# Hybrid GLA / sliding-window layer on one core: second FF product in groups of eight, decayed keys made earlier, and a new order at two Strassen seams

## The chip, the core and the metric

The kernel runs on one core of a Trainium2 chip. TensorE (PE) multiplies, VectorE (DVE), ScalarE (ACT) and GpSimd (POOL) do the elementwise work, SyncE (SP) issues every DMA. The metric is the time of one execution in microseconds of device time; the figure for a kernel is the median of its runs.

## What is computed

One decoder layer over 2048 tokens of width 1024, in float32, with 16 learned meta tokens ahead of them:

```python
u = rmsnorm(h, norm_mix_w); proj = u @ w_in
o_gla = gla_mixer(gq, gk, gv, gr, glr, ...)   # 4 heads, gated linear attention in chunks
o_swa = swa_mixer(sq, sk, sv, sinks, pos)     # 8 heads, window 128, 16 meta keys, a sink
h = h + concat([o_gla, o_swa]) @ w_out
f = rmsnorm(h, norm_ff_w)
h = h + square(relu(f @ w_ff1)) @ w_ff2       # 1024 -> 4096 -> 1024
return rmsnorm(h, final_norm_w)
```

Within a chunk of GLA the state is S = exp(b_last) S + sum over j of (k_j exp(b_last - b_j)) v_j. The factor k_j exp(b_last - b_j) is what the kernel calls the decayed keys.

## The kernel before

**Layout.** Activations lie transposed, 128 features on the partitions and 512 tokens (a block, `NB`) along the free axis; four blocks make up the 2048 tokens. Every dense product is done in split precision: an operand x is kept as a rounded part h and a rest l = x - h, and `mm3` issues three matmuls (wh·ah, wl·ah, wh·al; lines 160, 161, 162) where one would do. Weights arrive as 128x1024 tiles (`raw`, 512 KB); ACT makes `wh`, DVE `wl` (`split_w`, lines 125 and 126). A product of K row tiles is 3K matmuls of 512 columns into one PSUM bank (`psd`, three banks in rotation).

**Stages in order.** (1) `in_proj`, blocks 0 and 1, then 2 and 3. (2) `trunk(0)` and `trunk(1)`: output projection, first FF product (`up`, 32 FF tiles), second FF product (`down`). (3) `tail_pair`, blocks 2 and 3 together: the output projections, then in `tail_ordered` a cover of dense work and the first FF product by a Strassen scheme of seven products per 2x2 of tiles (operands `ops[1..7]`), 16 rounds j of seven slots, 12 matmuls a slot. (4) the class `Second`: the second FF product by the same scheme, 49 steps of 24 matmuls. (5) `last_down`, a plain remainder, and the final norm.

**What runs beside the dense work.** From stage 1 into stage 2 two generators are advanced once per `yield` of the dense code: `gla` (chunks of 128 tokens) and `swa`. Their matmuls stand among the dense ones on PE; a scheduler that plans ahead of time decides the order on each engine up to the end of the output projections of stage 3. Each engine runs its list in order, so a PE instruction that waits holds all that stand behind it. A GLA chunk makes seven levels (`gla_level`, `gla_level_mm`; `kl`, `ql`, `lv`), whose key tiles alternate between two buffers `kl[0]` and `kl[1]`; the decayed keys are put into `kl[1]` too, after the last level.

**The FF pair.** `up(ff)` writes one hidden tile pair; `down(g)` multiplies a group of four of them for all eight output tiles m and adds each product to the residual `hs[m]` on DVE (line 863). The pairs live in a pool `hb` of five units. In the last group of block 0 and the sixth of block 1 the inputs of the next output projection are loaded and split as well (`ahead`, `load_mix`).

**The cover and the first Strassen rounds.** The last eight FF tiles of block 1 (`hid6`, `hid7`) are not used in `trunk(1)`. `tail_ordered` multiplies them in 16 products of 12 matmuls, and under this cover DVE and ACT build the first Strassen operands from a list `chain`, in pieces that `work(us)` hands out by nominal DVE costs (1.23 us for a 128x1024 subtraction). From here to the end the order on every engine is the order of the code (`manual_schedule`). The products of a round go to four banks b0 to b3. Line 1264 forms c11 = s + b2; slot 6 of the round accumulates into b2 again, so its first matmul waits for that read.

**The second product.** `Second` has a table of jobs by step (`job(at, ...)`). `prepare(s)` makes `wh` and `bh` on ACT, `wl` and `bl` on DVE; it runs two steps ahead, for steps 0 and 1 inside the last Strassen round (`before(slot)`). A step works on four PSUM banks, one after another, `psw`: three of the pool that also holds b0 and b2 (`pd`), one of `px`. `close_0` (line 1195) is the last read of the last round's b2. `load_acc` loads the residual sums `c21`, `e`, `f`, `c11`; `sum_acc` forms f = e - f and e = e - c21.

Of the kernel before, what the change touches and what calls it, by code (L numbers as in the profile page):

```python
# [35 lines left out]
class Layer:  # L36
# [546 lines left out]
    def decayed_keys(self, gp, B, k, n):  # L583

        nc = self.nc
        kt = self.kl[1][:, :, :n]
# [100 lines left out]
    def gla_chunk(self, b, gp, qk, v):  # L687
# [30 lines left out]
        kt = self.decayed_keys(gp, B, k, P)  # L718
        yield
        kT = self.transpose_keys(gp, kt, P)  # L720
# [96 lines left out]
    def trunk(self, blk, ahead_of, hid_pair, last):  # L817
# [14 lines left out]
        hid = [[None] * 4 for _ in range(8)]  # L832

        def up(ff):
# [10 lines left out]
            hid[ff // 4][ff % 4] = (h, l)  # L845
# [9 lines left out]
        def down(g):  # L855
            if g == 7:
                accs[0] = self.acc_tile()
            for mp in range(4):
                w = self.split_w(a["w2"][g, mp].rearrange("p m k c -> p (m k c)"))
                for mi in range(2):  # L860
                    m = 2 * mp + mi
                    ps = yield from self.product(w, lambda k: hid[g][k], 4, 4 * mi)
                    nc.vector.tensor_tensor(hs[m], hs[m], ps, ALU.add)  # L863
                    if g == 7:
                        self.sumsq_add(hs[m], accs[0], m, fast=True)
                    if g == (5 if last else 7) and m >= 4:
                        self.ahead = self.ahead or ahead_of()
                        for _ in range(3):
                            next(self.ahead[0], None)
                    yield  # L870

        yield from up(0)
        for g in range(8):
            for t in range(1, 4):
                yield from up(4 * g + t)
            if g < 7:
                yield from up(4 * g + 4)
            if last and g >= 6:
                continue
            self.half_way = last and g >= 5  # L880
# [5 lines left out]
        if last:  # L886
            self.left = hs, units, hid[6], hid[7]
# [4 lines left out]
    def tail_pair(self, blks, ax, hb, pq):  # L892
# [3 lines left out]
        hs1, units1, hid6, hid7 = self.left  # L896
# [58 lines left out]
        def cov_load(t):  # L955
            cov_raw[t] = self.wp.tile([P, 1024], F32, name="raw", tag="raw")
            nc.sync.dma_start(out=cov_raw[t], in_=a["w2"][6 + t // 4, t % 4].rearrange("p m k c -> p (m k c)"))
# [19 lines left out]
    def tail_ordered(  # L977
# [3 lines left out]
        hs1, units1, hid6, hid7 = self.left  # L981
# [130 lines left out]
        def cov_add(m, last, ps):  # L1112
            TT(hs1[m], hs1[m], ps, ALU.add)
            if last and m % 2:
# [565 lines left out]
```

## Time and profile before

| | |
|---|---|
| median of 3 runs | 2188.69 us (2186.64 to 2188.81) |
| the profiled execution, its own time | 2190.38 us |
| span of that execution, first to last instruction | 2188.7 us |
| mean granted TensorE clock | 0.994 of full speed |
| PE busy | 2149.2 us, 98% of the span |
| DVE busy | 1575.0 us, 72% |
| ACT busy | 1047.6 us, 48% |

Matmuls overlap: a 512-column matmul is shown as 0.39 us long, and the next one starts 0.227 us after it. So where PE runs without a gap its time is the number of matmuls, and the questions are where it stands idle and where the next start comes later than 0.227 us.

### The profile page before, as it was taken

Reading aid. Unit: us, or ns where it says so; the run is one execution under the profiler, and the core shown is the slowest. Engines: PE = TensorE matmul, PEld = TensorE weight load, DVE = VectorE, ACT = ScalarE, POOL = GpSimd, SP = SyncE. Lnnn points to the kernel's source line nnn. Section 1 sums busy time; section 2 is a strip of 40 time slices with the busy share of each in tenths; the row PEclk is TensorE's granted clock in tenths of the full one; section 3 lists DMA queues with packets and bytes.
Section 4 is the critical chain, followed back from the end, with each engine's and each line's share of the span. In section 5 each row is a group of like instructions: output and inputs, shape, how many; then the busy total and the mean of one; then the engine's idle time right before and its main releaser. Section 6 shows DMA issues by size and latency. Waiting matters only on the chain.

```text
span 2188.7 us, 29186 instructions
## 1 busy us (share of the span) xinstructions
PE 2149.2 (98%) x10423; PEld 1804.3 (82%) x10423; DVE 1575.0 (72%) x2927; ACT 1047.6 (48%) x2156; POOL 193.7 (9%) x311
## 2 busy tenths in 40 slices
PE   8999999999999999999999999999999999999997
PEld 6998789788888888887888888888788887888886
DVE  6167774988988888889974445566867775775866
ACT  5132754456665556667553323453544444333434
POOL 2000110121221111221110000000000000000001
PEclk9999999999999999999999999999999999999999
DMA  6234533335333333334333334553355557654412
GB/s 205 96 98 133 152 112 110 100 114 171 109 104 99 103 110 109 106 102 146 126 100 98 96 97 146 176 166 129 119 162 176 169 197 251 254 173 144 154 39 77
DMA packets 146801, 291.47 MB, mean 133 GB/s; under 512 B 12256, under 2 KB 63968, under 8 KB 146656
## 3 DMA queue, kind: packets, MB, share of 16 engines
q1 hardware_dynamic: 146656, 289.61, 41.4%
q8 instruction: 82, 1.34, 0.3%
q14 instruction: 63, 0.52, 0.1%
HBM read 219.63 MB, written 69.86 MB: 132 GB/s over the span
## 4 chain that ended last, share of the span: by engine, by line
PE 84%; DVE 8%; ACT 4%; DMA 2%; issue 1%; POOL 0%; DVEq 0%; SPq 0%; ACTq 0%; POOLq 0%
PE psd L161 15%; PE psd L160 15%; PE psd L162 15%; PE psq L160 4%; PE psq L161 4%; PE psq L162 4%; PE psw L160 4%; PE psw L162 4%; PE psw L161 4%; PE lv L677 2%; PE psd L295 2%; PE psd L296 2%; PE psd L297 2%; PE pv L530 1%; ACT p L479 1%
## 5 line engine op out<-in xcount | busy, mean ns | idle before, releaser
L125 ACT ACTIVATE wh<-raw 128x1024 fp32r<-128x1024 f32 (+2 forms) x190 | 199.2, 1048 | 322.6 <-PE psd L162 279.6
L126 DVE TENSOR_TENSOR wl<-raw,wh 128x1024 fp32r<-128x1024 f32 (+2 forms) x190 | 233.9, 1231 | 75.3 <-ACT wh L125 74.4
L160 PE MATMUL psd<-hid,wh 128*128 128x512 f32 x512 | 203.7, 398 | 0.2 <-ACT hid L843 0.2
L160 PE MATMUL psd<-f,wh 128*128 128x512 f32 x512 | 202.7, 396 | 0.0
L162 PE MATMUL psd<-f,wh 128*128 128x512 f32 x512 | 200.2, 391 | 0.0
L161 PE MATMUL psd<-f,wl 128*128 128x512 f32 x512 | 199.9, 390 | 0.0
L161 PE MATMUL psd<-hid,wl 128*128 128x512 f32 x512 | 199.8, 390 | 0.0
L162 PE MATMUL psd<-hid,wh 128*128 128x512 f32 x512 | 199.6, 390 | 0.0
L160 PE MATMUL psd<-u,wh 128*128 128x512 f32 x416 | 169.2, 407 | 4.9 <-DVE st L241 3.2
L161 PE MATMUL psd<-u,wl 128*128 128x512 f32 x416 | 164.7, 396 | 1.0 <-DVE wl L126 1.0
L162 PE MATMUL psd<-u,wh 128*128 128x512 f32 x416 | 165.0, 397 | 0.3 <-DVE u L156 0.2
L160 PE MATMUL psw<-bh,wh 128*128 128x512 f32 x392 | 153.2, 391 | 2.1 <-DVE su L1195 2.1
L161 PE MATMUL psw<-bh,wl 128*128 128x512 f32 x392 | 153.2, 391 | 0.0
L162 PE MATMUL psw<-bl,wh 128*128 128x512 f32 x392 | 153.1, 391 | 0.0
L161 PE MATMUL psq<-oh,wl 128*128 128x512 f32 x384 | 149.5, 389 | 0.8 <-DVE wl L963 0.8
L162 PE MATMUL psq<-ol,wh 128*128 128x512 f32 x384 | 149.6, 390 | 0.6 <-DVE ol L913 0.6
L160 PE MATMUL psq<-oh,wh 128*128 128x512 f32 x384 | 149.8, 390 | 0.0
L962 ACT ACTIVATE wh<-rw 128x1024 fp32r<-128x1024 f32 x49 | 52.0, 1061 | 150.5 <-PE psw L162 134.3
L863 DVE TENSOR_TENSOR h<-h,psd 128x512 f32<-128x512 f32 x112 | 76.6, 684 | 61.4 <-PE psd L162 61.1
L162 PEld LDWEIGHTS psd<-f,wh 128*128 128x128 f32 x512 | 96.1, 188 | 21.1 <-DVE f L156 0.4
L162 PEld LDWEIGHTS psd<-hid,wh 128*128 128x128 f32 x512 | 96.1, 188 | 20.6
L160 PEld LDWEIGHTS psd<-hid,wh 128*128 128x128 f32 x512 | 96.2, 188 | 19.7 <-ACT hid L843 0.4
(315 smaller groups left out, 5229.4 us busy)
## 6 DMA issues: line engine op xcount, KB each, us to landing
raw<-w SPq DMA_DIRECT2D x132, 512.0 KB, 3.6
b<-hops SPq DMA_DIRECT2D x49, 512.0 KB, 3.5
raw<-wo SPq DMA_DIRECT2D x32, 512.0 KB, 4.0
r<-w SPq DMA_DIRECT2D x32, 512.0 KB, 4.0
rw<-w2q SPq DMA_DIRECT2D x28, 512.0 KB, 5.5
raw<-wf SPq DMA_DIRECT2D x26, 512.0 KB, 3.7
feat<-st SPq DMA_DIRECT2D x52, 256.0 KB, 2.2
hops<-t SPq DMA_DIRECT2D x42, 256.0 KB, 5.0
```

The source lines that it names most:

```text
L125: nc.scalar.activation(wh, raw, AF.Copy)
L126: nc.vector.tensor_tensor(wl, raw, wh.bitcast(F32), ALU.subtract)
L160: nc.tensor.matmul(ps, lhsT=wh, rhs=ah, start=first, stop=False, skip_group_check=skip)
L161: nc.tensor.matmul(ps, lhsT=wl, rhs=ah, start=False, stop=False, skip_group_check=skip)
L162: nc.tensor.matmul(ps, lhsT=wh, rhs=al, start=False, stop=last, skip_group_check=skip)
L295: nc.tensor.matmul(ps, lhsT=ah, rhs=wh, start=kt == 0, stop=False)
L296: nc.tensor.matmul(ps, lhsT=ah, rhs=wl, start=False, stop=False)
L297: nc.tensor.matmul(ps, lhsT=al, rhs=wh, start=False, stop=kt == KT - 1)
L479: nc.scalar.activation(p[:, g, win], p[:, g, win], AF.Exp, bias=nm[:, g : g + 1], accum_out=sm[:, g : g + 1])
L677: nc.tensor.matmul(ps[:, hp * P : (hp + 1) * P], lhsT=kl[:, hp, :], rhs=ql[:, :, hp, :], start=True, stop=True)
L863: nc.vector.tensor_tensor(hs[m], hs[m], ps, ALU.add)
L962: nc.scalar.activation(wh, src, AF.Copy)
```

## The change

Four edits, of which the first alters the weights' layout, too:

1. `down` works on groups of eight FF tiles (24 matmuls into one bank, one addition to `hs[m]`) instead of four; the cover does the same with `hid3`, the last eight tiles, one output tile at a time. Nine hidden pairs live at once: five in `hb`, four in the pool of the activations (`ap_`).
2. The decayed keys get a tile of their own and are made at level 3 and transposed at level 5, no longer behind level 6.
3. In the cover, `work` hands out 0.80 and 2.72 us in turn where it handed out 0.80 and 2.03.
4. In the second product, `prepare` is cut into a high and a low half. In the last Strassen round the low half of step 0 comes after the reads of slot 5, that of step 1 after `close_0`. The four banks of a set are taken in the order pd, pd, px, pd (before: pd, pd, pd, px). The loads of `e`, `f` move from step 0 to steps 5 and 7, `c11` from 5 to 4; a copy `x` of the original `c21` is loaded at step 6 into `hb`, and `sum_acc` moves from steps 2 and 3 to 12 and 13.

```diff
     def decayed_keys(self, gp, B, k, n):
-        kt = self.kl[1][:, :, :n]
+        kt = gp.tile([P, 2, P], F32, name="kt", tag="g", bufs=1)[:, :, :n]
...
             yield
+            if li == 3:
+                kt = self.decayed_keys(gp, B, k, P)
+            elif li == 5:
+                kT = self.transpose_keys(gp, kt, P)
             self.gla_level_mm(li, AT, *lv[li])
...
-        kt = self.decayed_keys(gp, B, k, P)
         yield
-        kT = self.transpose_keys(gp, kt, P)
         yield
...
         def down(g):
...
-            for mp in range(4):
-                w = self.split_w(a["w2"][g, mp].rearrange("p m k c -> p (m k c)"))
-                for mi in range(2):
-                    m = 2 * mp + mi
-                    ps = yield from self.product(w, lambda k: hid[g][k], 4, 4 * mi)
-                    nc.vector.tensor_tensor(hs[m], hs[m], ps, ALU.add)
...
+            for m in range(KT):
+                w = self.split_w(a["w2"][g, m].rearrange("p k c -> p (k c)"))
+                ps = yield from self.product(w, lambda k: hid[g][k])
+                nc.vector.tensor_tensor(hs[m], hs[m], ps, ALU.add)
+                if g == 3:
+                    self.sumsq_add(hs[m], accs[0], m, fast=True)
+                if g == (2 if last else 3) and m >= 4:
...
         for i in range(16):
-            g, m = i // 8, i % 8
+            m, half = i // 2, i % 2
...
-            for k, (h, l) in enumerate((hid6, hid7)[g]):
...
+            for k in range(4 * half, 4 * half + 4):
+                c = slice(k * P, (k + 1) * P)
+                self.mm3(ps, wh[:, c], wl[:, c], *hid3[k], k == 0, k == 7)
...
-                work(2.72 - 0.69 - (1.23 if i % 2 == 0 else 0))
+                work(2.72 - (1.92 if half == 0 else 0))
...
         close_0(old)
+        W2.prepare_lo(1)
...
-                    lambda ff: self.pair("hid", F32R, self.ap_ if ff >= 29 else hb),
+                    lambda ff: self.pair("hid", F32R, hb if ff % 9 < 5 else self.ap_),
...
         self.job(-4, self.load_acc, "c21", 0, 1)
-        self.job(0, self.load_acc, "e", 1, 1)
-        self.job(0, self.load_acc, "f", 1, 0)
+        self.job(5, self.load_acc, "e", 1, 1)
+        self.job(6, self.load_acc, "x", 0, 1, hb)
+        self.job(7, self.load_acc, "f", 1, 0)
+        self.job(4, self.load_acc, "c11", 0, 0)
+        for s in range(2, len(self.steps)):
+            self.job(s - self.AHEAD, self.prepare, s)
...
-            self.job(2, self.sum_acc, "f", "e", "f", u)
-            self.job(3, self.sum_acc, "e", "e", "c21", u)
...
+            self.job(12, self.sum_acc, "f", "e", "f", u)
+            self.job(13, self.sum_acc, "e", "e", "x", u)
...
+        if slot == -4:
+            self.prepare_hi(0)
+        elif slot == -2:
+            self.prepare_lo(0)
+            self.prepare_hi(1)
...
-                banks[i].append(lay.px.tile([P, NB], F32, name="psw", tag="sx"))
+                banks[i].insert(2, lay.px.tile([P, NB], F32, name="psw", tag="sx"))
...
-    A["w2"] = f["w_ff2"][0].reshape(8, 4, P, 4, 2, P).transpose(0, 3, 2, 4, 1, 5)
+    A["w2"] = f["w_ff2"][0].reshape(4, 8, P, KT, P).transpose(0, 3, 2, 1, 4)
```

In the program that results, the list of PE holds the same number of each kind of matmul; DVE's holds 64 fewer additions of 128x512 (96 instead of 160 of the form h<-h,psd), SP's two more loads.

**Place 1: the transposes of the decayed keys (`kT`) in the fifth of 17 calls, during the in-projection of blocks 2 and 3.** On DVE, before:

```order
L682 COPY_PREDICATED AT<-lmask,lv 128x256
L717 TENSOR_TENSOR qB<-qk,eB 128x256
L587 TENSOR_TENSOR kl_123<-B 128x256
L126 TENSOR_TENSOR wl<-raw,wh 128x1024
L589 TENSOR_TENSOR kl_123<-kl_123,qk 128x256
```

and with the change, where the level of size 4 stands around it:

```order
L587 TENSOR_TENSOR kt<-B 128x256
L659 TENSOR_TENSOR E<-B 128x256
L663 TENSOR_TENSOR kl_122<-qk,E 128x32x4
L667 TENSOR_TENSOR ql<-qpad,E 128x256
L589 TENSOR_TENSOR kt<-kt,qk 128x256
L243 TENSOR_TENSOR st<-psd,rb 128x512
```

On PE `kT` stood between two matmuls of the sliding window, 15 matmuls behind the last level's `lv`; now it stands ahead of the level of size 2, at least 12 dense matmuls behind the `lv` that reads the `ql` above:

```order
L160 MATMUL psd<-u,wh 128x512
L161 MATMUL psd<-u,wl 128x512
L162 MATMUL psd<-u,wh 128x512
L596 MATMUL kT<-tabs,kt 128x128 x2
L677 MATMUL lv<-ql,kl_123 128x128 x2
```

**Place 2: DVE from the end of the cover into the first Strassen round.** L1113 is the cover's addition, L913 makes the low part `ol` of an operand, L1046 and L1049 are sums of operands, L963 is a `wl`. Before, from the last addition to the read of b2 (L1264):

```order
L1113 TENSOR_TENSOR h<-h,psd 128x512
L1046 TENSOR_TENSOR h<-h 128x1024
L963 TENSOR_TENSOR wl<-x,wh 128x1024
L913 TENSOR_TENSOR ol<-t_14343,oh 128x1024
L1046 TENSOR_TENSOR h<-h 128x1024
L913 TENSOR_TENSOR ol<-t_14384,oh 128x1024
L963 TENSOR_TENSOR wl<-r,wh 128x1024
...
```

With the change the same pieces begin ahead of the last addition (the second L1113 here):

```order
L1046 TENSOR_TENSOR h<-h 128x1024
L1113 TENSOR_TENSOR h<-h,psd 128x512
L963 TENSOR_TENSOR wl<-x,wh 128x1024
L913 TENSOR_TENSOR ol<-t_14221,oh 128x1024
L1046 TENSOR_TENSOR h<-h 128x1024
L1113 TENSOR_TENSOR h<-h,psd 128x512
L913 TENSOR_TENSOR ol<-t_14260,oh 128x1024
L963 TENSOR_TENSOR wl<-r,wh 128x1024
...
```

Behind these, on either side, follow two L1049, L1026, L1255 (now L1256), one L963 and several L913 (before five, now six: one has moved up from behind the pair), and then the pair L1263, L1264 (now L1264, L1265).

**Place 3: DVE at the seam of the two Strassen products.** L1263 and L1264 (now L1264, L1265) read the banks of slots 4 and 5, L1195 (now L1196) the last bank b2; L963 and L1562 (now L1567) are the low halves of `prepare`. Before:

```order
L963 TENSOR_TENSOR wl<-rw,wh 128x1024
L1562 TENSOR_TENSOR bl<-b,bh 128x1024
L1263 TENSOR_TENSOR su<-su,psq 128x512
L1264 TENSOR_TENSOR cc<-su,psq 128x512
L963 TENSOR_TENSOR wl<-rw,wh 128x1024
L1562 TENSOR_TENSOR bl<-b,bh 128x1024
L1266 TENSOR_TENSOR su<-su,psq 128x512
L1161 SCALAR_TENSOR_TENSOR h_16621<-h_16621,vecs,rb 128x512
L1195 TENSOR_TENSOR su<-su,psq 128x512
```

Now:

```order
L1264 TENSOR_TENSOR su<-su,psq 128x512
L1265 TENSOR_TENSOR cc<-su,psq 128x512
L963 TENSOR_TENSOR wl<-rw,wh 128x1024
L1567 TENSOR_TENSOR bl<-b,bh 128x1024
L1267 TENSOR_TENSOR su<-su,psq 128x512
L1162 SCALAR_TENSOR_TENSOR h_16510<-h_16510,vecs,rb 128x512
L1196 TENSOR_TENSOR su<-su,psq 128x512
L963 TENSOR_TENSOR wl<-rw,wh 128x1024
L1567 TENSOR_TENSOR bl<-b,bh 128x1024
```

The reads of the two banks moved ahead of all low halves, and the low half of step 1 behind the read of b2.

## Rows read from the trace of the kernel before

**Rows 1.** Page, part 1: busy us (share of the span) and instructions of each engine

```profile
PE 2149.2 (98%) x10423; PEld 1804.3 (82%) x10423; DVE 1575.0 (72%) x2927; ACT 1047.6 (48%) x2156; POOL 193.7 (9%) x311
```

**Rows 2.** Waits of PE, whole span: line, releaser, us in total, times, longest

```profile
PE kT L596 <- DVE kl L589: 4.8, 3, 3.0
...
PE psq L160 <- DVE cc L1264: 2.7, 2, 1.3
PE psw L160 <- DVE su L1195: 2.1, 1, 2.1
...
PE psq L161 <- DVE wl L963: 0.8, 1, 0.8
PE psq L162 <- DVE ol L913: 0.6, 1, 0.6
```

**Rows 3.** Windows: stretch, length, busy us of PE, PEld, DVE, ACT, POOL, clock, DMA

```profile
380.00:440.00 60.00, 56.20 (x287) 46.62 (x287) 56.92 (x139) 26.65 (x81) 10.75 (x18) 1.00 0.34 106
...
1000.00:1050.00 50.00, 46.86 (x232) 37.54 (x231) 47.91 (x104) 33.66 (x86) 8.52 (x16) 1.00 0.54 181
...
1545.00:1565.00 20.00, 18.04 (x71) 13.70 (x70) 19.90 (x22) 12.49 (x16) 0.00 (x0) 0.91 0.18 53
...
1845.00:1865.00 20.00, 16.50 (x65) 12.84 (x64) 10.22 (x11) 9.56 (x12) 0.00 (x0) 0.91 0.85 301
1865.00:2145.00 280.00, 280.00 (x1237) 231.91 (x1236) 201.38 (x205) 105.53 (x110) 0.00 (x0) 1.00 0.42 145
```

**Rows 4.** Timeline around the longest kT wait: start us, us, engine, line, operation, idle before

```profile
424.80 0.41 DVE L589 TENSOR_TENSOR kl<-kl,qk 128x256 f32<-128x256 f32 x1
...
425.36 0.41 PE L596 MATMUL kT<-tabs,kl 128*128 128x128 f32 x2 [2.99 <-DVE kl L589]
```

**Rows 5.** Groups by line, DVE: operation, shapes, count, busy us, mean ns, idle before

```profile
L863 DVE TENSOR_TENSOR h<-h,psd 128x512 f32<-128x512 f32 x112 | 76.6, 684 | 61.4 <-PE psd L162 61.1
```

**Rows 6.** Waits of PE, 60 to 1100 us (columns as in rows 2)

```profile
PE pv L530 <- POOL ph L523: 1.0, 1, 1.0
PE oT L766 <- DVE o L739: 0.9, 1, 0.9
```

**Rows 7.** Timeline of the first Strassen round, PE and DVE (columns as in rows 4)

```profile
1544.16 1.22 DVE L913 TENSOR_TENSOR ol<-t,oh 128x1024 fp32r<-128x1024 f32 x1
...
1556.71 2.36 DVE L913 TENSOR_TENSOR ol<-h,oh 128x1024 fp32r<-128x1024 f32 x2
1558.98 0.69 DVE L1263 TENSOR_TENSOR su<-su,psq 128x512 f32<-128x512 f32 x1
1559.70 0.69 DVE L1264 TENSOR_TENSOR cc<-su,psq 128x512 f32<-128x512 f32 x1
...
1560.54 0.57 PE L160 MATMUL psq<-oh,s 128*128 128x512 f32 x1 [1.35 <-DVE cc L1264]
1560.90 0.63 PE L161 MATMUL psq<-oh,s 128*128 128x512 f32 x1
...
1563.46 0.63 PE L161 MATMUL psq<-oh,s 128*128 128x512 f32 x1
```

**Rows 8.** Timeline at the seam of the two Strassen products (columns as in rows 4)

```profile
1847.63 1.23 DVE L1562 TENSOR_TENSOR bl<-b,bh 128x1024 fp32r<-128x1024 f32 x1 [3.25 <-PE psq L162]
...
1850.23 0.50 PE L160 MATMUL psq<-oh,s 128*128 128x512 f32 x1 [1.35 <-DVE cc L1264]
...
1856.02 0.68 DVE L1195 TENSOR_TENSOR su<-su,psq 128x512 f32<-128x512 f32 x1
...
1856.76 0.50 PE L160 MATMUL psw<-bh,wh 128*128 128x512 f32 x1 [2.15 <-DVE su L1195]
...
1857.84 0.63 PE L161 MATMUL psw<-bh,wl 128*128 128x512 f32 x1
...
1860.39 0.63 PE L161 MATMUL psw<-bh,wl 128*128 128x512 f32 x1
```

**Rows 9.** Page, part 6, a DMA of 2 KB runs: count, KB each, median us to landing

```profile
rw<-w2q SPq DMA_DIRECT2D x28, 512.0 KB, 5.5
```

More of the change, by code (lines that the diff above doesn't have):

```diff
@@ L831, in trunk @@
         rb = []
-        hid = [[None] * 4 for _ in range(8)]
+        hid = [[None] * 8 for _ in range(4)]
         def up(ff):
@@ L855, in down @@
         def down(g):
-            if g == 7:
+            if g == 3:
                 accs[0] = self.acc_tile()
-            for mp in range(4):
-                w = self.split_w(a["w2"][g, mp].rearrange("p m k c -> p (m k c)"))
-                for mi in range(2):
-                    m = 2 * mp + mi
-                    ps = yield from self.product(w, lambda k: hid[g][k], 4, 4 * mi)
-                    nc.vector.tensor_tensor(hs[m], hs[m], ps, ALU.add)
[L864 to L870, printed above, removed]
-        yield from up(0)
[L873 to L878, printed above, removed]
+            for m in range(KT):
+                w = self.split_w(a["w2"][g, m].rearrange("p k c -> p (k c)"))
+                ps = yield from self.product(w, lambda k: hid[g][k])
+                nc.vector.tensor_tensor(hs[m], hs[m], ps, ALU.add)
+                if g == 3:
+                    self.sumsq_add(hs[m], accs[0], m, fast=True)
+                if g == (2 if last else 3) and m >= 4:
+                    self.ahead = self.ahead or ahead_of()
+                    for _ in range(3):
+                        next(self.ahead[0], None)
+                yield
+        yield from up(0)
+        for g in range(4):
+            for t in range(1, 8):
+                yield from up(8 * g + t)
+            if g < 3:
+                yield from up(8 * g + 8)
+            if last and g == 3:
                 continue
-            self.half_way = last and g >= 5
+            self.half_way = last and g == 2
             yield from down(g)
@@ L886, in trunk @@
         if last:
-            self.left = hs, units, hid[6], hid[7]
+            self.left = hs, units, hid[3]
         else:
@@ L1134, in tail_ordered @@
                 cov_add(*adds)
-            adds = (m, g, ps)
+            adds = (m, ps) if half else None
             if i % 2 == 0 and i // 2 + 1 < 8:
@@ L1475, in __init__ @@
         self.job(-4, self.load_acc, "c21", 0, 1)
-        self.job(0, self.load_acc, "e", 1, 1)
-        self.job(0, self.load_acc, "f", 1, 0)
-        for u in range(2):
-            self.job(2, self.sum_acc, "f", "e", "f", u)
-            self.job(3, self.sum_acc, "e", "e", "c21", u)
-        self.job(5, self.load_acc, "c11", 0, 0)
-        for s in range(len(self.steps)):
-            self.job(s - self.AHEAD, self.prepare, s)
+        self.job(5, self.load_acc, "e", 1, 1)
[4 more added lines that the diff above has]
+            self.job(s - self.AHEAD, self.prepare, s)
+        for u in range(2):
+            self.job(12, self.sum_acc, "f", "e", "f", u)
+            self.job(13, self.sum_acc, "e", "e", "x", u)
         self.hid, self.ws, self.raw = [None] * 4, [None] * 8, {}
```

43 lines of the change are left out of this document (23 added, 20 removed).

## The prediction, made before the changed kernel ran

> **What bounds the kernel now.** I read the table of engines first. PE is busy 98% of the span [rows 1], so only idle time of PE or slow matmuls can be won back; the change leaves PE's matmul counts alone. In a stretch without a gap, 1237 matmuls take 280 us [rows 3], 0.227 us from start to start; a slot of 12 is then 2.72 us, a product of 24 is 5.45.
>
> Then the waits of PE. The three groups that stand behind the edited code are the transposes of the decayed keys, 4.8 us in three waits; the read of b2 by the line of c11, 2.7 us in two waits, one in the first Strassen round and one at the seam of the two Strassen products; and the last read of b2 by `close_0`, 2.1 us. Two smaller ones of 0.8 and 0.6 us, for a `wl` and an `ol`, belong to the first round [rows 2].
>
> Then the two places by windows and timeline. In both the mean granted clock is 0.91, where the unbroken stretch behind them has 1.00 [rows 3]. The timelines say when: behind the wait of 1.35 us in the first round the matmuls start 0.43 us apart (1560.90 to 1563.46 is six steps), and so they do behind the 2.15 us wait at the seam (1857.84 to 1860.39, six steps) [rows 7, 8]. That is close to twice 0.227, the lower of the engine's two levels, 1.2 instead of 2.4 GHz. So a wait there costs more than its own length. With the one or two starts ahead of and behind those shown, I put seven steps in the round and eight at the seam, at 0.20 us each too long: 1.4 and 1.6 us.
>
> **A. Decayed keys.** The longest of the three waits shows the mechanism: the last multiplication (L589) starts on DVE at 424.80, ends at 425.21, and the transposes start at 425.36 after 2.99 us of idling [rows 4]. Each of PE's instructions behind them, dense ones too, is held as long. With the change the keys are finished two levels earlier (place 1). PE reaches the `lv` that uses the `ql` one operation ahead of L589 at least 12 dense matmuls, 2.7 us, before the transposes, so whatever holds L589 holds that `lv` first, and L589 takes 0.41 us more [rows 4]. Nothing is queued behind the transposes that was not queued behind that `lv`. The work is the same; the new tile costs nothing but space. Bounds 0 and 4.8 us [rows 2]. Around the longest wait DVE is busy 56.92 of 60 us [rows 3], so part of the lateness may show up at another wait: I take 4.0.
>
> **B. Groups of eight.** 64 of the additions to `hs[m]` or to the cover's sums go, each 684 ns [rows 5]: 43.8 us of DVE. For most of it DVE is hidden behind PE. Where both run tight is 1000 to 1050, the second FF product of block 1 with the last sliding-window work beside it: DVE is busy 47.91 of 50 us, PE 46.86 [rows 3], and PE waits there for a multiplication of POOL (1.0) and for an output of DVE (0.9) [rows 6]. Some three additions are gone there, 2 us of DVE, in a stretch where PE stands 3.1 us idle: bounds 0 and 3, and I take 1.5. What it adds: nine hidden pairs are alive at once and a product takes 5.45 instead of 2.72 us, hence fewer hand-overs; I see no wait for a place in the pools.
>
> A rule of the Trainium skill speaks against this term. "Perfetto Trace Analysis", section "Identifying the Most-Contended Engine", says to take the engine with the highest occupancy as the one to improve. By it the engine is TensorE, VectorE with its 72% over the span [rows 1] is not, and this term is nothing. The windows show VectorE the busier of the two in that one stretch [rows 3], which a share over the span can't show. By the page the sum is 1.5 us smaller, by the row it is as below.
>
> **C. The cover and the first round.** Before: waits of 1.35 (c11), 0.77 and 0.62 us, 2.7 together [rows 2, 7], and 1.4 of slow matmuls: 4.1. DVE is full there, 19.90 of 20 us [rows 3], so the wait for c11 can only shrink if DVE's pieces begin earlier. The new budget lets them (place 2). How far? The `ol` at 1544.16 (operand 5) needs a place in `hb`, and now all eight hidden pairs are read until the cover's end: the pair whose place it takes is read last by the seventh matmul from the end, which starts 7 × 0.227 = 1.59 us before the end and lasts 0.39. So the piece begins about 1.1 us before the cover's end, T0. From its start to the end of the c11 line it took 1560.39 − 1544.16 = 16.23 us before [rows 7]. Now one more L913 stands in that stretch (2.27 / 2 = 1.135 us by the start of the pair at 1556.71 and of L1263 behind it [rows 7]), and the cover's last addition (0.69): 18.06 us, to T0 + 16.95. Slot 6 is due 72 × 0.227 = 16.35 us after T0. A wait of 0.6 us remains, and I count on the small ones to vanish and on the clock to hold: 4.1 − 0.6 = 3.5. Bounds 0 and 4.1.
>
> **D. The seam.** Before: waits of 1.35 and 2.15, and 1.6 of slow matmuls [rows 8]: 5.1. The first is a queueing error: DVE made `bl` of the next product at 1847.63, which had to wait for PE to release its place, while the two reads for c11, ready to run, stood behind it [rows 8]. Now the reads come first (place 3). They need slot 4's bank, complete 2.72 us before slot 6 is due, and take 0.69 each: about 1.1 us of margin. Behind them `wl` and `bl` of step 0, 1.23 each, are done 2.46 − 1.1 = 1.4 us into slot 6, and step 0 needs the first of them 2.72 + 0.23 us into it, 1.6 us later. The second wait: `close_0` is no longer behind the second `wl` and `bl`; it can start as slot 6 ends and takes 0.68 [rows 8], with the last matmul's tail some 0.9 us. The bank that it frees was the third of step 0, needed after 6 matmuls; it is now the fourth, needed after 9, 2.04 us. Margin 1.1 us. The low half of step 1 comes behind, 2.5 us of DVE, with 4.5 us left. So the residue is 0 and the gain 5.1. Were one of the two margins missed, the clock would fall as before: bounds 2.0 and 5.1.
>
> **What is moved elsewhere.** The loads of `e`, `f`, `c11` and the extra `x` leave SP behind other loads of the second product, where PE runs 280 us without a wait and DVE is busy 201 of them [rows 3]; `sum_acc` brings four pieces of 1.23 us to steps 12 and 13, behind `prepare`, which is two steps (10.9 us) ahead. The new layout of w2 gives four late weight loads runs of 2 KB; a DMA of such runs lands in 5.5 us [rows 9] and is issued five steps (27 us) ahead. Nothing for all of these.
>
> **Sum.** 4.0 + 1.5 + 3.5 + 5.1 = 14.1. The scheduler redraws the order of both mixers' work around A, and where one instruction waits less another can wait more: I take 1.0 off. 13.1 us less than the profiled execution's own 2190.4 gives 2177.3. That execution stands 1.7 us above the median, so the median should be 2175.6. A measurement of this kernel can tell about 0.2%, 4.4 us, from no change.
>
> **Rivals.**
> - R1, VectorE is the bound in the mixers' stretch: what A and B free comes back at other waits, both are 0 and the allowance with them. For: 95 and 96% busy there [rows 3]. Against: only the last instruction of a chain moved. The gain is 8.6, the time 2180.1.
> - R2, the round stays as it was: the places in `hb` are held until T0, so DVE starts no earlier and the wait and the slow matmuls stay. For: the margin in C is already missed by 0.6. Against: the order does move two pieces ahead. Gain 13.1 − 3.5 = 9.6, time 2179.1.
> - R3, slower: the transposes, two levels earlier, wait for the exponential and the multiplication of their keys in each of the 16 full chunks, not in three. Then A is lost and 16 waits of w come on top: with 9.1 left of the sum the kernel is slower than before from w = 9.1 / 16 = 0.57 us, and by 0.2% from (9.1 + 4.4) / 16 = 0.84 us. At w = 1.5, half of the 2.99 [rows 4], it is 24 − 9.1 = 14.9 us slower, 2203.6. Against: at least 12 dense matmuls stand between, and the `lv` ahead of them needs the same DVE queue.
> - R4, the additions are worth nothing, as the page's rule has it: gain 11.6, time 2177.1.
> - R5, no change: DVE is the bound on both sides, in the mixers' stretch (R1) and at both seams (R2, and one margin of D missed), so that only the 2.0 of D's lower end is left: 2186.7.
>
> **How the numbers follow.** The forecast with its own range, 2171.7 to 2178.4 (A to D between 0.8 of their values and their upper bounds; 0.8 × 14.1 − 1.0 = 10.3), has 0.50; R1 0.14, R2 0.12, R4 0.12, R5 0.07, R3 0.05. Down, the upper bounds give 4.8 + 3 + 4.1 + 5.1 = 17.0, 2171.7; I go to 2169.5 for waits nearby that shrink too. Up, R1, R2 and R4 lie inside 2183, which leaves R5, R3 and a little of the tails outside: the range is 2169.5 to 2183. Faster by over 0.2% is the forecast, R1, R2 and R4, 0.88; within 0.2% R5, 0.07; slower R3, 0.05.
>
> **What the profile will show.** A right: no wait of PE for L589, and no new one for the `E` or `ql` lines beside it. B right: fewer than 3 us of idle PE in the window that was 1000 to 1050. C right: at most 0.6 us for c11 in the first round, clock near 1.00 in its window; wrong: 1 us or more and matmuls 0.43 apart. D right: no wait of PE between the last round and step 1, clock 1.00; wrong: a wait for `close_0` or `bl`. Wrong as a whole if PE waits often for `kT` or its keys, or if SP's later loads make the 280 us stretch show a gap.

## Result

The changed kernel takes 2171.64 us (median of 6 runs, 2170.22 to 2172.48), against 2188.75 us for the one before in the same comparison: a ratio of 0.9922, 95% interval 0.9909 to 0.9935, so 17.1 us or 0.8% less. The prediction was 2175.6 us, with a range of 2169.5 to 2183; the sum of the terms was 13.1 us. The result lies inside the stated range and 0.06 us below the forecast's own, narrower one (2171.7 to 2178.4), and it came about in another way than forecast: one term was much too large and one much too small, and the errors cancelled in part.

The profiled execution after took 2170.22 us. The table of engines of its page:

```profile
PE 2141.0 (99%) x10423; PEld 1801.7 (83%) x10423; DVE 1537.9 (71%) x2863; ACT 1046.4 (48%) x2156; POOL 198.8 (9%) x311
```

PE has the same 10423 matmuls as in [rows 1]; DVE has 64 instructions and 37 us less. The waits of PE over the span, columns as in [rows 2]:

```profile
PE psd L161 <- DVE wl L126: 3.0, 2, 2.0
...
PE psq L160 <- DVE cc L1265: 0.5, 1, 0.5
```

The waits for L589 are gone, and so are those for `close_0`, for the `wl` and the `ol` of the first round and one of the two for c11. What is new is the first line: 3.0 us for a `wl` of `split_w`, where before there were 1.6. The windows that answer to [rows 3] (the program now runs some 10 us ahead at the first Strassen round and some 15 at the seam):

```profile
400.00:425.00 25.00, 23.05 (x110) 18.77 (x109) 24.79 (x53) 6.99 (x19) 5.01 (x9) 0.96 0.23 75
1000.00:1050.00 50.00, 49.98 (x252) 41.94 (x252) 46.37 (x97) 31.32 (x77) 12.34 (x18) 1.00 0.55 175
1535.00:1555.00 20.00, 19.46 (x87) 15.81 (x85) 19.08 (x23) 12.73 (x17) 0.00 (x0) 1.00 0.21 68
1835.00:1855.00 20.00, 20.00 (x90) 16.57 (x89) 12.24 (x13) 11.22 (x13) 0.00 (x0) 1.00 1.00 370
1855.00:2135.00 280.00, 279.63 (x1266) 232.39 (x1264) 203.91 (x213) 106.67 (x117) 2.59 (x2) 1.00 0.40 137
```

PE is full from 1000 to 1050 (49.98 instead of 46.86 us) and at the seam (20.00 of 20), and the first round has 0.54 us left. In 400 to 425 it still stands 2 us idle, and the granted clock is 0.96 there (before, 1.00 from 380 to 440). The 0.37 us missing in the last window are a wait of the remainder behind the second product (L160 for L1336), which the kernel before has too; the second product itself shows no gap.

Idle time alone misses what a slow or late start costs. So I also took, for both traces, the time from each matmul's start to the next one's, less the median of that time for matmuls of the same line, operand names and shape in the same execution, and added it up by stretch. This "lost time" of PE, in us:

| stretch (us of the span) | before | after | won | term, predicted |
|---|---|---|---|---|
| 0 to 100, not touched by the change | 12.2 | 9.2 | 3.0 | none |
| 100 to 1000, the mixers | 14.4 | 13.1 | 1.2 | A, 4.0 |
| 1000 to 1100, end of block 0, next output projection | 7.1 | 1.4 | 5.7 | B, 1.5 |
| 1500 to 1600, first Strassen round | 5.8 | 0.7 | 5.1 | C, 3.5 |
| 1800 to 1900, the seam | 5.6 | −0.1 | 5.7 | D, 5.1 |
| the rest | 7.6 | 7.7 | −0.1 | none |
| sum from 100 us on (of unrounded figures) | 40.4 | 22.8 | 17.6 | 13.1 with the allowance |

The sum without the first 100 us, 17.6, is close to the 17.1 of the medians; the first 100 us differ from execution to execution (8.5 to 12.2 us in the fourteen traces of this study) and explain why the two profiled executions lie 20.2 us apart.

The borders of the stretches blur three figures. The third wait for L589 falls into the row of B, with 0.7 us of its 5.7, though the prediction counts it under A (it is gone as well in experiments 2, 6 and 7, which have the old keys):

```profile
1019.19 0.41 PE L596 MATMUL kT<-tabs,kl 128*128 128x128 f32 x2 [0.54 <-DVE kl L589]
```

Of the 5.8 us of the first round 0.4 belong to a start at 1501.9 us, well ahead of the round, which after the change stands at 1491.7 us and so counts in the rest; the round itself went from 5.4 to 0.7. And the row of A holds, after the change, some 1.4 us of slow starts (0.43 us apart instead of 0.227) behind the wait at 420 us, which the execution before did not have.

**Around 420 us**, PE, DVE and POOL in the timeline after:

```profile
419.96 0.39 PE L160 MATMUL psd<-u,wh 128*128 128x512 f32 x1
420.00 0.67 DVE L721 TENSOR_TENSOR qB<-qk,eB 128x256 f32<-128x256 f32 x1
420.35 0.82 POOL L523 TENSOR_SCALAR_AFFINE_SELECT pl<-pl 128x512 fp32r<-128x512 f32 x1
420.60 1.65 DVE L126 TENSOR_TENSOR wl<-raw,wh 128x1024 fp32r<-128x1024 f32 x1
...
422.30 0.50 PE L161 MATMUL psd<-u,wl 128*128 128x512 f32 x1 [1.95 <-DVE wl L126]
...
423.11 1.21 DVE L126 TENSOR_TENSOR wl<-raw,wh 128x1024 fp32r<-128x1024 f32 x1
423.41 0.63 PE L162 MATMUL psd<-u,wh 128*128 128x512 f32 x1
423.83 0.63 PE L160 MATMUL psd<-u,wh 128*128 128x512 f32 x1
```

At the place where PE waited 2.99 us for the keys [rows 4], it now waits 1.95 us for the `wl` that stood just ahead of L589 in DVE's queue before. From 423.41 on seven matmuls start 0.43 us apart.

**First round**, answering to [rows 7]:

```profile
1529.07 1.22 DVE L913 TENSOR_TENSOR ol<-t,oh 128x1024 fp32r<-128x1024 f32 x1 [0.84 <-PE psd L162]
...
1530.16 0.39 PE L160 MATMUL psq<-oh,wh 128*128 128x512 f32 x1
...
1539.96 4.62 DVE L913 TENSOR_TENSOR ol<-h,oh 128x1024 fp32r<-128x1024 f32 x4
1544.50 1.22 DVE L963 TENSOR_TENSOR wl<-r,wh 128x1024 fp32r<-128x1024 f32 x1
1545.64 0.68 DVE L1264 TENSOR_TENSOR su<-su,psq 128x512 f32<-128x512 f32 x1
1546.35 0.69 DVE L1265 TENSOR_TENSOR cc<-su,psq 128x512 f32<-128x512 f32 x1
...
1547.19 0.47 PE L160 MATMUL psq<-oh,s 128*128 128x512 f32 x1 [0.54 <-DVE cc L1265]
1547.49 0.39 PE L161 MATMUL psq<-oh,s 128*128 128x512 f32 x1
```

The first line is the `ol` of operand 5: it waits for a matmul of the cover and starts 1.09 us ahead of the round's first matmul at 1530.16. The wait for c11 is 0.54 us where 0.6 were reckoned, and the next start follows at 0.30 us, not at 0.43. **The seam**, answering to [rows 8]:

```profile
1831.26 0.69 DVE L1264 TENSOR_TENSOR su<-su,psq 128x512 f32<-128x512 f32 x1 [6.75 <-PE psq L162]
1831.98 0.69 DVE L1265 TENSOR_TENSOR cc<-su,psq 128x512 f32<-128x512 f32 x1
...
1833.82 1.23 DVE L1567 TENSOR_TENSOR bl<-b,bh 128x1024 fp32r<-128x1024 f32 x1
...
1836.50 0.39 PE L160 MATMUL psw<-bh,wh 128*128 128x512 f32 x1
1836.70 0.69 DVE L1196 TENSOR_TENSOR su<-su,psq 128x512 f32<-128x512 f32 x1 [0.39 <-PE psq L162]
...
1838.54 0.39 PE L160 MATMUL psw<-bh,wh 128*128 128x512 f32 x1
```

Step 0 begins at 1836.50 without a gap, `close_0` ends at 1837.39, and the tenth matmul, the first on its bank, comes at 1838.54: a margin of 1.15 us, where the prediction had 1.1.

### The profile page after: what moved, and what is told of

Same layout as the page of the kernel before. It is cut to its first block, busy times and chain, and to the rows that moved or that the text cites. A ratio compares the mean times of both kernels' runs of the same rounds, so it can differ in the third digit from the quotient of the medians.

```text
span 2168.5 us, 29105 instructions
## 1 busy us (share of the span) xinstructions
PE 2141.0 (99%) x10423; PEld 1801.7 (83%) x10423; DVE 1537.9 (71%) x2863; ACT 1046.4 (48%) x2156; POOL 198.8 (9%) x311
## 4 chain that ended last, share of the span: by engine, by line
PE 87%; DVE 7%; ACT 3%; DMA 1%; issue 1%; DVEq 0%; SPq 0%; ACTq 0%
PE psd L162 16%; PE psd L161 16%; PE psd L160 16%; PE psq L160 4%; PE psq L162 4%; PE psq L161 4%; PE psw L160 4%; PE psw L161 4%; PE psw L162 4%; PE lv L677 2%; PE psd L295 2%; PE psd L296 2%; PE psd L297 2%; PE pv L530 1%; DVE wl L126 1%
## 5 line engine op out<-in xcount | busy, mean ns | idle before, releaser
L126 DVE TENSOR_TENSOR wl<-raw,wh 128x1024 fp32r<-128x1024 f32 (+2 forms) x190 | 234.0, 1232 | 74.5 <-ACT wh L125 73.9
L160 PE MATMUL psd<-f,wh 128*128 128x512 f32 x512 | 203.2, 397 | 0.0
L160 PE MATMUL psd<-hid,wh 128*128 128x512 f32 x512 | 202.9, 396 | 0.0
L160 PE MATMUL psd<-u,wh 128*128 128x512 f32 x416 | 167.7, 403 | 3.7 <-DVE st L241 2.4
L160 PE MATMUL psw<-bh,wh 128*128 128x512 f32 x392 | 152.5, 389 | 0.0
L160 PE MATMUL psq<-oh,wh 128*128 128x512 f32 x384 | 149.8, 390 | 0.0
L160 PEld LDWEIGHTS psd<-hid,wh 128*128 128x128 f32 x512 | 96.2, 188 | 19.3 <-issue 0.2
L161 PEld LDWEIGHTS psd<-hid,wl 128*128 128x128 f32 x512 | 96.2, 188 | 19.1 <-issue 0.2
```

Source lines behind the costliest of these rows:

```text
L126: nc.vector.tensor_tensor(wl, raw, wh.bitcast(F32), ALU.subtract)
L160: nc.tensor.matmul(ps, lhsT=wh, rhs=ah, start=first, stop=False, skip_group_check=skip)
L161: nc.tensor.matmul(ps, lhsT=wl, rhs=ah, start=False, stop=False, skip_group_check=skip)
```

## Experiments

All were timed against the kernel before; a time here is the median of the runs. "Lost" is the lost time of PE as above.

### 1 and 2. The decayed keys alone, and the change without them

Experiment 1 puts edit 2 alone into the kernel before; experiment 2 takes it out of the changed kernel. The lines are the same, here for experiment 2:

```diff
-        kt = gp.tile([P, 2, P], F32, name="kt", tag="g", bufs=1)[:, :, :n]
+        kt = self.kl[1][:, :, :n]
...
-            if li == 3:
-                kt = self.decayed_keys(gp, B, k, P)
-            elif li == 5:
-                kT = self.transpose_keys(gp, kt, P)
...
+        kt = self.decayed_keys(gp, B, k, P)
         yield
+        kT = self.transpose_keys(gp, kt, P)
         yield
```

> The kernel before with edit 2 alone (decayed keys at level 3, transposes at level 5). Theory 1, term A as predicted: the three waits for L589 (4.8 us) go and little comes back, 4.0 us less, about 2184.7 us. Theory 2, VectorE's queue is late as a whole around 420 us, so PE waits there for the next thing that it wants of VectorE (a wl, 2 us or more): only the waits at 590 and 1019 us are won, 1.0 to 2.0 us less, about 2187.2 us, and the stretch 400 to 450 us keeps 3 us or more of lost PE time.

Measured: 2185.09 us against 2187.63 (ratio 0.9988, 0.9979 to 0.9997), 2.5 us less. Lost in 400 to 450: 4.6 us (before 3.8), in 450 to 1000: 3.8 (5.4), in 1000 to 1100: 3.6 (7.1).

> The changed kernel with edit 2 undone. Theory 1 (A is worth 4.0): 2175.6 us, with PE waits for L589 of 4 us or more. Theory 2 (the wait only moves): 2172.5 to 2173.5 us, and the waits for L589 that come back are paid for by the waits for a wl that go.

Measured: 2170.22 us (0.9921, 0.9908 to 0.9935), no slower than the changed kernel. The waits of PE and, at the place, its timeline:

```profile
PE kT L596 <- DVE kl L589: 4.2, 2, 3.0
...
PE psd L161 <- DVE wl L126: 1.0, 1, 1.0
```

```profile
422.01 0.43 PE L596 MATMUL kT<-tabs,kl 128*128 128x128 f32 x2 [2.99 <-DVE kl L589]
```

The waits for L589 are back at 4.2 us, and 2.0 us of waits for a `wl` have gone. Lost from 100 to 1000: 5.3 + 5.5 + 4.1 = 14.9, against 13.1 in the changed kernel. So theory 2 holds for the place at 420: PE waits there for whatever it wants next of DVE, whose queue is late as a whole (24.79 of 25 us busy). In lost time edit 2 is worth some 2 us in 100 to 1000 (14.9 against 13.1; of traces without slow starts behind the wait at 420, 13.1 in experiment 7 against 11.2 and 10.8 in experiments 8 and 10). The medians don't show it: experiment 2 is 1.4 us below the changed kernel and so below the times of both theories, and in experiment 1 the gain of 2.5 us lies between theory 1 (4.0) and theory 2 (1.0 to 2.0). Those 2.5 us come for the most part from the end of block 0, where edit 1 brings the same.

### 3 and 4. The additions put back; the inputs packed again

```diff
                 nc.vector.tensor_tensor(hs[m], hs[m], ps, ALU.add)
+                nc.vector.tensor_tensor(hs[m], hs[m], hs[m], ALU.max)
```

> The changed kernel with a second VectorE operation of 128x512 behind every addition to hs in the second FF product (56 more, a maximum of a tile with itself, which leaves the values as they are), so that VectorE has its old load in groups of eight. Theory 1 (term B is VectorE's time for the additions): 4 to 5 us come back, about 2176 us, with the waits of PE at the end of block 0. Theory 2 (what counts is that the last four products of the block, between which the next block's inputs are split, are twice as long, so that this work is spread over 21.8 us in place of 10.9): within 1.5 us of the changed kernel, about 2172.5 us.

Measured: 2171.87 us (0.9929, 0.9916 to 0.9943). Lost in 1000 to 1100: 2.4 us (changed kernel 1.4), from 450 to 1000: 4.2 (3.2).

```diff
-                if g == (2 if last else 3) and m >= 4:
+                if g == (2 if last else 3) and m >= 6:
                     self.ahead = self.ahead or ahead_of()
-                    for _ in range(3):
+                    for _ in range(6):
```

> The changed kernel with the splitting of the next block's inputs (ahead) put into the last two products of the group, six pieces each, in place of four products with three: 10.9 us as before the change. Theory 1 (the additions' time): no more than 1 us slower, about 2172 us. Theory 2 (the spreading): 3 to 5 us slower, 2175 to 2177 us, with PE waits for VectorE or GpSimd behind the end of block 0.

Measured: 2169.40 us (0.9919, 0.9905 to 0.9932), lost in 1000 to 1100: 1.6 us. Neither edit brings the 5.7 us back; the additions are worth about 1 us of lost time in this stretch and 0.2 us of the median (that they are worth another 1.0 from 450 to 1000 is not shown: experiment 5 below, which has them too, has 3.4 there), the longer stretch for the inputs nothing by itself. Both theories of 3 and 4 fail as the one cause.

### 5, 6 and 7. What makes the waits at the end of block 0

Experiment 5 has the edits of 3 and 4 together. Experiment 6 spreads the inputs in the kernel before:

```diff
-                    if g == (5 if last else 7) and m >= 4:
+                    if g == (5 if last else 7) and m >= 2:
                         self.ahead = self.ahead or ahead_of()
-                        for _ in range(3):
+                        for _ in range(2):
```

Experiment 7 is the kernel before with edit 1: the hunks of `down`, of the cover and of w2 from the change's diff, with the old budget, which in the new cover reads

```diff
-                work(2.72 - 0.69 - (1.23 if i % 2 == 0 else 0))
+                work(2.72 - 0.69 - (1.23 if half == 0 else 0))
```

> The changed kernel with both edits of e3_additions_back and e4_inputs_packed: the second VectorE operation behind every addition and the next block's inputs split within 10.9 us. Theory 1 (VectorE is full at the end of block 0 only when additions and inputs meet there): 3 to 5 us slower than the changed kernel, 2174.5 to 2176.5 us, and 4 us or more of lost PE time in 1000 to 1100 us. Theory 2 (the waits of before were those of one particular order of the instructions, which any redrawing loses): no more than 2.5 us lost there, about 2172 us.

> The kernel before with one thing changed: the splitting of the next block's inputs is put into six products of the group, two pieces each, in place of four with three, so over 16.4 us in place of 10.9. Theory 1 (VectorE's load at the end of block 0): 2 to 4 us less, 2183.5 to 2185.5 us. Theory 2 (one particular order): some gain or none, and the waits of 1000 to 1100 us at other instructions than before.

> The kernel before with edit 1 alone (groups of eight, in the cover too; the cover's old budget, the old keys and the old seam of the two products). If term B stands by itself and is as large as the two profiles make it: 5 to 6 us from the stretch 1000 to 1100 us, and 0 to 1.5 us in the first Strassen round, since the order there is nearly that of before: 2180 to 2182.5 us. If the stretch needs edit 2 as well (the key's wait and the order behind it): 2183 us or more.

Measured: experiment 5 2172.46 us (0.9929, 0.9917 to 0.9942); experiment 6 2181.33 (0.9975, 0.9966 to 0.9984); experiment 7 2179.37 (0.9960, 0.9947 to 0.9972). Lost in 1000 to 1100: 3.2, 2.6 and 1.2 us. The window of 1000 to 1050 us, columns as in [rows 3], of experiment 1,

```profile
1000.00:1050.00 50.00, 48.48 (x242) 40.04 (x241) 49.05 (x105) 35.06 (x85) 14.45 (x18) 1.00 0.57 191
```

of 5,

```profile
1000.00:1050.00 50.00, 49.47 (x249) 40.81 (x248) 48.51 (x104) 33.16 (x80) 11.87 (x18) 1.00 0.62 202
```

of 6,

```profile
1000.00:1050.00 50.00, 49.72 (x251) 41.32 (x250) 48.95 (x104) 34.75 (x83) 11.01 (x18) 1.00 0.53 185
```

and of 7:

```profile
1000.00:1050.00 50.00, 49.98 (x252) 41.68 (x251) 46.40 (x100) 31.55 (x77) 11.92 (x18) 1.00 0.53 174
```

Before, DVE was busy 47.91 us there and PE 46.86 [rows 3]. In experiments 5 and 6 DVE is busier still, 48.5 and 49.0 us, and PE hardly stands idle. So DVE's load in the window alone is not what cost the 7.1 us. Three unlike edits each remove half of it or more, alone: the earlier keys 3.4 us, the inputs over six products 4.4, groups of eight 5.8. The gains don't add. The time of experiment 5 is that of theory 2, but its 3.2 us of lost time lie between the two theories (4 or more, 2.5 at most); experiment 6 gained 5.8 us where theory 1 gave 2 to 4, and its waits are at other instructions, as theory 2 said; experiment 7 came 0.6 us below its range. On the whole that speaks for theory 2: the waits belonged to one order of the instructions, and the planner draws another after each of these edits.

For the wait for POOL [rows 6] the traces show which place it was. Near 1036 us before, the matmul `pv<-ph,vd`, which reads `ph` behind POOL's mask (L523), has only four PE instructions between it and `pv<-ph,vc`, which reads `ph` ahead of the mask, and the mask takes 1.50 us:

```profile
1035.38 0.50 PE L530 MATMUL pv<-ph,vc 128*128 128x512 f32 x1
...
1036.59 1.50 POOL L523 TENSOR_SCALAR_AFFINE_SELECT ph<-ph 128x512 fp32r<-128x512 f32 x1 [19.59 <-DVE pl L514]
...
1038.14 0.50 PE L530 MATMUL pv<-ph,vd 128*128 128x512 f32 x1 [0.95 <-POOL ph L523]
```

In all thirteen other traces 41 instructions stand between the two and this matmul does not wait; in experiment 6:

```profile
1035.54 0.51 PE L530 MATMUL pv<-ph,vc 128*128 128x512 f32 x1
...
1044.67 0.48 PE L530 MATMUL pv<-ph,vd 128*128 128x512 f32 x1
```

The wait for `o` [rows 6] is not of this kind: its place on PE is the same in every trace compared, and it comes back with 0.85 us in experiment 1 and 0.23 in experiment 5. What makes it and the smaller waits there come and go was not isolated.

### 8. The cover's old budget

```diff
-                work(2.72 - (1.92 if half == 0 else 0))
+                work(2.72 - 0.69 - (1.23 if half == 0 else 0))
```

> The changed kernel with edit 3 undone (the cover hands out 0.80 and 2.03 us in turn). Theory 1, term C as predicted: the early start of VectorE's pieces is the budget's work, the wait for c11 in the first round comes back at 1.0 us or more with matmuls 0.43 us apart behind it, 2.5 to 4 us slower, 2174 to 2176 us. Theory 2, the eight additions fewer in the cover give VectorE the time: no more than 0.7 us slower, 2172.3 us or less.

Measured: 2174.41 us (0.9937, 0.9925 to 0.9949), 2.8 us above the changed kernel; lost in the first round 4.4 us against 0.7. PE and DVE in its timeline:

```profile
1549.05 0.47 PE L160 MATMUL psq<-oh,s 128*128 128x512 f32 x1 [1.35 <-DVE cc L1265]
...
1552.15 0.50 PE L162 MATMUL psq<-ol,s 128*128 128x512 f32 x1 [1.01 <-DVE ol L913]
```

```profile
1545.22 2.36 DVE L913 TENSOR_TENSOR ol<-h,oh 128x1024 fp32r<-128x1024 f32 x2
...
1550.88 1.22 DVE L913 TENSOR_TENSOR ol<-h,oh 128x1024 fp32r<-128x1024 f32 x1
```

The wait of 1.35 us is back to the hundredth, and so is that of 0.62 us for the `ol` ahead of it. Theory 1 holds: the budget is what moves the pieces forward. The eight additions fewer give 0.7 us by themselves: they shorten the wait of 0.77 us for a `wl` early in the round to 0.10, here, and 0.11 in experiment 7. The slow matmuls expected behind the wait don't come in this execution. In their place PE waits 1.01 us for the sixth `ol`, which with the old budget stands behind the reads for c11 (place 2). Before, the slow matmuls of 1.4 us stood there and this wait does not show; in experiment 6, whose round is that of before, it shows with 1.01 us and without slow matmuls, and the round loses 5.1 us all the same.

### 9, 10 and 11. The seam

Experiment 9 makes `prepare` whole again for steps 0 and 1, experiment 10 moves one line, and experiment 11 the bank:

```diff
-        for s in range(2, len(self.steps)):
+        for s in range(len(self.steps)):
             self.job(s - self.AHEAD, self.prepare, s)
```

```diff
-        close_0(old)
         W2.prepare_lo(1)
+        close_0(old)
```

```diff
-                banks[i].insert(2, lay.px.tile([P, NB], F32, name="psw", tag="sx"))
+                banks[i].append(lay.px.tile([P, NB], F32, name="psw", tag="sx"))
```

(In experiment 9 the calls of `prepare_hi` and `prepare_lo` in `before` and behind `close_0` are gone.)

> The changed kernel with prepare whole again for steps 0 and 1, as before (the fourth place of b2's bank stays). Term D's theory: the low half of step 0 stands ahead of the reads for c11 again, a wait of 1.35 us; that of step 1 ahead of close_0, a wait of 2.15 less the three matmuls by which the bank is now needed later (0.68), 1.5 us. 2.9 us of waits, and 1.6 us more if the matmuls behind them start 0.43 us apart: 2174.5 to 2176.2 us. Rival (the bank's place alone does it): no more than 1.5 us slower.

> The changed kernel with only the low half of step 1 ahead of close_0 instead of behind it. Term D's theory: 2.3 us of VectorE ahead of close_0 against a margin of 1.1 us: a wait of 0.8 to 1.2 us of PE for close_0, and no other; 2172.4 to 2173 us, up to 2174.5 if slow matmuls follow. Rival: VectorE had idle time enough ahead of close_0 (0.39 us were seen), no wait.

> The changed kernel with b2's bank the third of the four again. Term D's theory has a margin of 1.1 us less three matmuls, 0.4 us, so nothing is lost: 2171.6 us, no wait for close_0. Rival, the place in the order is needed: a wait for close_0 of 0.3 us or more, and the slow matmuls behind it.

Measured: experiment 9 2174.05 us (0.9937, 0.9923 to 0.9950); experiment 10 2168.86 (0.9912, 0.9899 to 0.9926); experiment 11 2170.39 (0.9922, 0.9909 to 0.9934). Lost at the seam: 3.4, 0.8 and −0.1 us. The waits of PE in experiment 9,

```profile
PE psq L160 <- DVE cc L1265: 1.9, 2, 1.3
PE psw L160 <- DVE su L1196: 1.5, 1, 1.5
```

in experiment 10,

```profile
PE psw L160 <- DVE su L1196: 0.5, 1, 0.5
```

and DVE around `close_0` in experiment 11:

```profile
1835.18 0.75 DVE L1162 SCALAR_TENSOR_TENSOR h<-h,vecs,rb 128x512 f32<-128x512 f32 x1
1836.31 0.69 DVE L1196 TENSOR_TENSOR su<-su,psq 128x512 f32<-128x512 f32 x1 [0.39 <-PE psq L162]
```

Experiment 9 gives both waits in the sizes reckoned, 1.3 (the rest of 1.9 is the first round's 0.54) and 1.5; no slow starts follow, and its time is 0.5 us below the range given. Experiment 10 shows 0.53 us of idle time where 0.8 to 1.2 were expected; by the starts the delay is 0.69, close to the 0.73 that is left of the 2.27 us of the low half when DVE's 0.39 us of idle time ahead of `close_0` and the margin of 1.15 are taken off. Experiment 11 loses nothing. So the halves in their order are what won the seam; the bank's place is a margin that this kernel doesn't need. The time expected of experiment 10, 2172.4 us or more, was missed: its four runs, 2168.04 to 2169.72 us, all lie below the six of the changed kernel. Its trace has the wait, and loses 2.3 us less than the changed kernel's in 100 to 1000, where the programs have the same order and where the changed kernel's has 1.4 us of slow starts behind the wait at 420 and this one has none; its low time is no gain of its edit as far as the trace shows.

### 12. The sums at steps 2 and 3 again

```diff
-            self.job(12, self.sum_acc, "f", "e", "f", u)
-            self.job(13, self.sum_acc, "e", "e", "x", u)
+            self.job(2, self.sum_acc, "f", "e", "f", u)
+            self.job(3, self.sum_acc, "e", "e", "c21", u)
```

(The loads of `e`, `f` and `c11` go back to steps 0, 0 and 5, and that of `x` is left out.)

> The changed kernel with the sums of the residuals at steps 2 and 3 again, e and f loaded at step 0, c11 at step 5 and no copy x. The prediction put nothing on that move: 2171.6 us, no wait in the second product. Rival: with the low half of step 1 behind close_0, four more pieces of 1.2 us in steps 2 and 3 (or the loads at step 0) make a prepare late, and PE waits once or more for a wl or bl of steps 3 to 6, 0.5 us or more.

Measured: 2170.39 us (0.9918, 0.9905 to 0.9930), lost from 1800 us on as in the changed kernel. The move of the sums, the copy `x` and its two loads are worth nothing, as the prediction had it.

No version here is shown to beat the changed kernel: experiments 2, 4, 10, 11 and 12 have medians 1.2 to 2.8 us below it, and their ratios to the kernel before, each measured beside it, have intervals that overlap with its own.

## Why the prediction was right in the sum, and where it was wrong

The sum of 13.1 us against 17.1 is in part luck: A was 2.8 us too high and B 4.2 too low.

**A, 4.0 predicted, 1.2 measured.** The step that failed is the one that let "part of the lateness" come back at another wait and put only 0.8 us on it. The argument that whatever holds L589 holds the `lv` ahead of it looked at the mixer's own chain; the instruction that took the wait over is a dense matmul that reads a `wl` from the same queue. Of the three waits of [rows 2] the one of 2.99 us came back as 1.95, and seven slow starts behind it took more than the rest (400 to 450: lost 3.8 before, 4.8 after; without slow starts, 3.4 and 3.1 in experiments 8 and 10); the one of 1.24 at 590 was won; that of 0.54 at 1019, in the row of B, goes without edit 2 as well. The row to go by was there: DVE had 56.92 of 60 us [rows 3], so the delay belonged to the queue and not to L589. That is the first half of rival R1.

**B, 1.5 predicted, 5.7 measured.** Here the step mis-sized is also misread. The prediction called 1000 to 1050 the product of block 1; it is the end of block 0 and the output projection behind it (the splitting of the next inputs, L786, and the final norm, L852, stand in DVE's timeline there). What it called a multiplication of POOL is the mask of L523. It then bounded the gain by PE's idle time in the window, 3.1 us, and gave the additions half of that. Lost time in 1000 to 1100 was 7.1 us, since waits also fall behind 1050 and every one delays the next start by more than the idle time shown. The additions themselves are worth about 1 us there (experiment 3), near the 1.5; the rest came with the new order (experiments 5 to 7), 0.7 of it by the third wait for L589 and some 1.4 by the place of `pv<-ph,vd`. What moved the remaining waits stays open. The Trainium skill's rule that the prediction weighed ("Perfetto Trace Analysis", section "Identifying the Most-Contended Engine") would have put 0 on this term and 2177.1 us on the kernel; the stretch gave 5.7 us, so neither the span's occupancy nor the window's told its worth. The section behind it on that page of the Trainium skill, "Optimization Strategy", says to find the gaps of the engine within a regime and what releases each. Reading wait by wait would have served here, as experiments 5 and 6 show with DVE 97 and 98% busy and PE nearly without a gap.

**C, 3.5 predicted, 5.1 measured.** The mechanism held to the tenth: DVE's pieces began 1.1 us ahead of the cover's end, and 0.54 us of the c11 wait remained where 0.6 were reckoned. R2 is refuted, and experiment 8 shows that the budget is the cause. What was too small is the base of 4.1 us: it counted idle time, and each of the three waits costs 0.16 us more by the starts (the next start is due 0.227 us after the last one, while that matmul is shown 0.39 us long). The slow starts cost 1.7 and not 1.4, and 0.5 are starts 0.11 to 0.15 us late beside the small waits; with the 0.4 at 1501 that makes the 5.8.

**D, 5.1 predicted, 5.7 measured.** Right in place, cause and margin (1.15 us against 1.1), and experiment 9 brings back both waits in the reckoned sizes. The slow starts in it depend on the execution (the last section): without them the old seam loses 4.0 us, in experiments 6 and 7. The bank's place, which the prediction counted as part of the margin, is not needed.

**At nothing:** the moved sums and loads (experiment 12), and the packed weight loads, behind which no PE wait is seen.

**The other rivals.** R3 did not occur: in the profile after PE never waits for the keys. R5 needed waits at both seams, and the one left is 0.54 us.

## What to carry to other kernels

A wait for an engine whose queue is full all around it (24.79 of 25 us here) need not go when the one instruction that was waited for is moved: ask which of the waiting engine's next instructions reads from the same queue, and expect the wait there. Where both sides of a hand-over have time to spare, as at the seam, the order in the queue decides, and the waits can be worked out from a handful of rows to a tenth or two of a us. Lost time should be taken from start to start, not from idle time. Where a planner draws the order, small edits that have nothing in common can free the same waits; test each alone and with the others before their gains are added, and look how far a matmul stands behind the one whose operand another engine still has to treat.

## What the runs showed of the hardware

**A wait of the same length does not always cost the same.** Behind the wait of 1.9 to 2.0 us for the `wl` near 420 us, five to seven matmuls started 0.43 us apart (the lower clock level) in eight traces, the changed kernel's and those of experiments 1, 3, 4, 5, 9, 11 and 12, and none did in experiments 8 and 10. The wait of 2.9 to 3.0 us for the keys was followed by seven in experiment 2 and by none before and in experiments 6 and 7. In experiment 10:

```profile
423.55 0.50 PE L161 MATMUL psd<-u,wl 128*128 128x512 f32 x1 [2.02 <-DVE wl L126]
423.89 0.40 PE L162 MATMUL psd<-u,wh 128*128 128x512 f32 x1
424.12 0.39 PE L160 MATMUL psd<-u,wh 128*128 128x512 f32 x1
```

The starts behind it are 0.23 us apart. The wait of 2.15 us at the seam was followed by slow starts before (seven [rows 8]) and in experiment 1 (six), and by none in experiments 6 and 7, which have the same wait there. Each slow start costs 0.20 us, so one such wait costs 2.0 us or 3.4, and part of the first 100 us' scatter is of that kind (1 to 19 slow starts there). The Trainium skill, "TensorE: Matmul & The Clock Gate", Part 1, calls the number of slow matmuls at a kernel's start variable from run to run; the traces agree for the first 100 us, and show the same behind waits in mid-kernel. For the prediction this means that the slow matmuls in C and D, 1.4 and 1.6 us, were a property of the one execution profiled, to be taken with a chance. In D they come on top (5.6 us with them, 4.0 without); in C their absence brings out the wait for the sixth `ol` (5.4 with them, 5.1 without).

**DVE can slow down beside GpSimd.** In the timeline at 420 us the `wl` that PE waits for takes 1.65 us and the multiplication ahead of it 0.67, while GpSimd's selection runs; a `wl` just behind, with GpSimd idle, takes 1.21 us, and 128x256 multiplications elsewhere 0.41 (L589, [rows 4]). Over the whole trace after, the 139 `wl` of 128x1024 (L126) with GpSimd idle take 1.20 to 1.26 us; of the 39 beside a GpSimd instruction 16 take more than 1.3, up to 1.82. By these figures some 0.7 us of the 1.95 us wait arise there, an estimate.
